# Channel shuffle on one core: eight tiles of 64 KB a partition, permuted inside their slot in pieces of five pixels

## The chip, the core and the metric

The kernel runs on one core of a Trainium2 chip. The metric is device time in microseconds (us), the median of several runs. The profile is one execution of the program, taken by the hardware profiler; its times count from the span's start, at the first instruction. Two engines matter here: VectorE (DVE in the profile), which copies within the on-chip memory (SBUF, 128 partitions), and the 16 DMA engines, which move data between device memory and SBUF. Transfers are issued from two queues: SP issues the loads (q1 in the profile) and ACT issues the stores (q10).

## The reference

The input is a float32 array of 16 x 64 x 64 pixels with 256 channels each, 67.11 MB. The 256 channels of a pixel are 8 groups of 32; the reference transposes the two:

```python
x = x.reshape(batch, h, w, groups, channels_per_group)
x = x.transpose(0, 1, 2, 4, 3)
x = x.reshape(batch, h, w, c)
```

No arithmetic is done. Each pixel's 1 KB stays where it is; inside it, channel g*32 + j goes to place j*8 + g. There are 65,536 pixels, 512 for each partition.

## The kernel before

The pixels are taken in order, in slots. `_SLOTS` (line 12) lists the pixels that each partition gets in a slot: [4, 8], then [28], then twelve times [38], then [16]; 512 in all. The first slot has two parts, each other slot has one. A part of q pixels is a contiguous block of 128 x q pixels of the input, and `rows` cuts it so that each partition's q pixels are one contiguous row of q KB (38 KB in most slots).

For each slot the kernel takes an `in_tile` from a pool of two and an `out_tile` from a pool of three, both sized for 38 pixels (lines 46 and 47). For each part it

- loads the part into `in_tile` by one DMA from the SP queue (line 55),
- copies it into `out_tile` by one VectorE `tensor_copy` (line 57), which reads the source with the order of groups and channels exchanged (a hop of 32 elements between consecutive reads) and writes one contiguous run,
- stores `out_tile` by one DMA from the ACT queue (line 61).

The order on each engine is the order of the program (`manual_schedule`); waits between engines are semaphores that the framework places from the tiles' uses. A load waits until the copy that last read its `in_tile` is done; a copy waits for its load, and for the store that last read its `out_tile`; a store waits for its copy. So loads are released by copies, and the three buffers of `out_tile` keep the stores out of the loads' way.

Of the kernel before, what the change touches and what calls it, by code (L numbers as in the profile page):

```python
# [1 line left out]

# [4 lines left out]


F32 = mybir.dt.float32
P = 128  # L10

_SLOTS = [[4, 8], [28]] + [[38]] * 12 + [[16]]
_IN_BUFS = 2
_OUT_BUFS = 3


@with_exitstack
def kernel(
    ctx: ExitStack,
    tc: tile.TileContext,  # L20
    x: bass.AP,
    groups: bass.AP,
    out: bass.AP,
):
    nc = tc.nc
    b, h, w, c = x.shape
    G = int(groups)
    CPG = c // G
    assert G * CPG == c
    assert sum(map(sum, _SLOTS)) * P == b * h * w  # L30
    biggest = max(map(sum, _SLOTS))

    x_flat = x.rearrange("b h w c -> (b h w c)")
    out_flat = out.rearrange("b h w c -> (b h w c)")

    in_pool = ctx.enter_context(tc.tile_pool(name="in_pool", bufs=_IN_BUFS))
    out_pool = ctx.enter_context(tc.tile_pool(name="out_pool", bufs=_OUT_BUFS))

    def rows(flat, first, q):

        return flat[first * c : (first + P * q) * c].rearrange("(p f) -> p f", p=P)

    ctx.enter_context(tc.manual_schedule(engines=None))
    first = 0
    for parts in _SLOTS:
        in_tile = in_pool.tile([P, biggest * c], F32, name="in_tile")
        out_tile = out_pool.tile([P, biggest * c], F32, name="out_tile")
        at = 0
        pieces = []
        for q in parts:  # L50
            pieces.append((q, first, slice(at * c, (at + q) * c)))
            first += P * q
            at += q
        for q, start, cols in pieces:
            nc.sync.dma_start(out=in_tile[:, cols], in_=rows(x_flat, start, q))  # L55
        for q, start, cols in pieces:
            nc.vector.tensor_copy(  # L57
                out=out_tile[:, cols].rearrange("p (i j g) -> p i j g", j=CPG, g=G),
                in_=in_tile[:, cols].rearrange("p (i g j) -> p i j g", g=G, j=CPG),
            )  # L60
            nc.scalar.dma_start(
                out=rows(out_flat, start, q), in_=out_tile[:, cols]
            )


# [1 line left out]
_INS = ['x', 'groups']  # L67
_OUTS = [((16, 64, 64, 256), 'float32')]

_NUMBERS = {'groups': 8}  # L70


# [26 lines left out]
```

## Time and profile before

| what | value |
|---|---|
| median of 3 runs | 316.17 us (316.07 to 316.84) |
| span of the profiled execution | 314.4 us (its own time is not given beyond the span) |
| VectorE busy | 119.0 us in 16 copies (38% of the span) |
| loads, q1 | 2304 packets, 67.11 MB |
| stores, q10 | 2304 packets, 67.11 MB |
| mean rate over the span | 427 GB/s |
| copy of 38 pixels (128 x 9,728 elements) | 8791 ns |
| copy of 4 pixels (128 x 1,024 elements) | 1092 ns |
| load of 38 pixels, issue to landing | 37.0 us |
| store of 38 pixels, issue to landing | 42.6 us |

The first part of the page gives each engine's busy time. The second cuts the span into 40 equal slices, where a digit is the busy share in tenths. The third gives the DMA queues, with the time of their packets as a share of 16 engines' span. A group of instructions is read as: line, engine, operation, output and input with their shapes, how many; then busy us and mean ns of one; then the idle time of the engine just before them, and what ended it. The chain of waits is read as: start, length, what. A line of the windows gives the stretch, its length, busy time (and instructions) of DVE and POOL, the granted TensorE clock (TensorE is not used), the DMA share and GB/s.

### The profile page before, as it was taken

How to read it: one execution, taken by the hardware profiler on the slowest of the kernel's cores; microseconds unless marked ns; L12 is line 12 of the kernel's file. 1: busy time of each engine (PE TensorE's matmuls, PEld its weight loads, DVE VectorE, ACT ScalarE, POOL GpSimd, SP SyncE). 2: the span in 40 equal slices, each digit the busy share in tenths (PEclk: the TensorE clock that was granted, in tenths of full speed). 3: DMA queues.
4: the chain of work that ended last, by engine and by line, in shares of the span. 5: the costliest groups of instructions: out<-in, count | busy, mean ns of one | idle time of the engine just before them, and what ended most of it. 6: DMA issues, size and time to landing. Idle time of an engine off the chain costs nothing.

```text
span 314.4 us, 132 instructions
## 1 busy us (share of the span) xinstructions
DVE 119.0 (38%) x16; POOL 0.2 (0%) x4
## 2 busy tenths in 40 slices
DVE  2081907309109109019028028037046055065400
POOL 0000000000000000000000000000000000000000
DMA  7999999999999999999999999999999999999997
GB/s 317 405 441 416 435 416 483 401 465 406 450 421 446 426 436 436 401 470 396 475 396 475 396 470 401 470 401 470 401 450 421 446 426 436 436 417 450 429 421 321
DMA packets 4608, 134.22 MB, mean 427 GB/s; under 512 B 512, under 2 KB 512, under 8 KB 768
## 3 DMA queue, kind: packets, MB, share of 16 engines
q1 hardware_dynamic: 2304, 67.11, 49.8%
q10 hardware_dynamic: 2304, 67.11, 49.4%
HBM read 67.11 MB, written 67.11 MB: 427 GB/s over the span
## 4 chain that ended last, share of the span: by engine, by line
DMA 76%; DVE 19%; issue 0%; SPq 0%; DVEq 0%
DMA in_tile<-in_x_dram 76%; DVE out_tile L57 19%; SPq L55 0%; DVEq L57 0%
## 5 line engine op out<-in xcount | busy, mean ns | idle before, releaser
L57 DVE COPY out_tile<-in_tile 128x9728 f32<-128x9728 f32 (+4 forms) x16 | 119.0, 7440 | 179.4 <-DMA in_tile<-in_x_dram 179.4
L80 POOL MEMSET const-uint8-127<- 128x1 uint8 x1 | 0.1, 103 | 0.0
L80 POOL MEMSET const-bfloat16-1.0<- 128x1 bf16 x1 | 0.1, 102 | 0.0
L80 POOL MEMSET const-float32-1.0<- 128x1 f32 x1 | 0.1, 100 | 0.0
L80 POOL MEMSET const-float32-0.0<- 128x1 f32 x1 | 0.1, 99 | 0.2 <-issue 0.2
## 6 DMA issues: line engine op xcount, KB each, us to landing
in_tile<-in_x_dram SPq DMA_DIRECT2D x12, 4864.0 KB, 37.0
out_dram<-out_tile ACTq DMA_DIRECT2D x12, 4864.0 KB, 42.6
in_tile<-in_x_dram SPq DMA_DIRECT2D x1, 3584.0 KB, 14.7
out_dram<-out_tile ACTq DMA_DIRECT2D x1, 3584.0 KB, 30.9
in_tile<-in_x_dram SPq DMA_DIRECT2D x1, 2048.0 KB, 30.4
out_dram<-out_tile ACTq DMA_DIRECT2D x1, 2048.0 KB, 15.2
in_tile<-in_x_dram SPq DMA_DIRECT2D x1, 1024.0 KB, 5.4
out_dram<-out_tile ACTq DMA_DIRECT2D x1, 1024.0 KB, 25.0
```

The lines of the kernel that those rows point to most:

```text
L57: nc.vector.tensor_copy(out=out_tile[:, cols].rearrange("p (i j g) -> p i j g", j=CPG, g=G), in_=in_tile[:, cols].rearrange("p (i g j) -> ...
L80: nc = _bacc.Bacc("TRN2", target_bir_lowering=False, num_devices=1)
```

## The change

The slots become eight tiles of 64 pixels a partition, each loaded by one DMA (64 KB a partition, 8.39 MB) and stored by one. One pool of three slots replaces the two pools. A slot has room for 64 + 5 pixels, 69 KB a partition. The load puts the 64 pixels at pixel 5 and up. VectorE then permutes them inside the slot: each `tensor_copy` takes five pixels and writes them permuted five pixels lower, into room that is free or whose pixels earlier pieces have already read. A tile takes twelve pieces of five pixels (1,280 elements) and one of four (1,024 elements); each piece waits on VectorE's own semaphore for the piece before it. The store takes pixels 0 to 63 of the slot. The next load into a slot waits for the store out of it.

In all there are 8 loads in place of 16, 8 stores in place of 16, and 104 copies in place of 16. The order on SP is the eight loads, on ACT the eight stores, on VectorE the pieces tile by tile. The loads of tiles 0, 1 and 2 wait for nothing; the load of tile k+3 waits for the store of tile k. The source of a piece is 5 x 32 x 8 elements at hops of 256, 1 and 32; its destination is one run of 1,280.

```diff
-_SLOTS = [[4, 8], [28]] + [[38]] * 12 + [[16]]
-_IN_BUFS = 2
-_OUT_BUFS = 3
+_SLOTS = [[64]] * 8
+_BUFS = 3
+
+_SHIFT = 5
...
-    biggest = max(map(sum, _SLOTS))
+    room = max(map(sum, _SLOTS)) + _SHIFT
...
-    in_pool = ctx.enter_context(tc.tile_pool(name="in_pool", bufs=_IN_BUFS))
-    out_pool = ctx.enter_context(tc.tile_pool(name="out_pool", bufs=_OUT_BUFS))
+    pool = ctx.enter_context(tc.tile_pool(name="pool", bufs=_BUFS))
...
-        in_tile = in_pool.tile([P, biggest * c], F32, name="in_tile")
-        out_tile = out_pool.tile([P, biggest * c], F32, name="out_tile")
+        slot = pool.tile([P, room * c], F32, name="slot")
...
-            pieces.append((q, first, slice(at * c, (at + q) * c)))
+            pieces.append((q, first, at))
...
-        for q, start, cols in pieces:
-            nc.sync.dma_start(out=in_tile[:, cols], in_=rows(x_flat, start, q))
-        for q, start, cols in pieces:
-            nc.vector.tensor_copy(
-                out=out_tile[:, cols].rearrange("p (i j g) -> p i j g", j=CPG, g=G),
-                in_=in_tile[:, cols].rearrange("p (i g j) -> p i j g", g=G, j=CPG),
+        for q, start, at in pieces:
+            nc.sync.dma_start(
+                out=slot[:, (at + _SHIFT) * c : (at + _SHIFT + q) * c],
+                in_=rows(x_flat, start, q),
             )
+        for q, start, at in pieces:
+            for lo in range(at, at + q, _SHIFT):
+                n = min(_SHIFT, at + q - lo)
+                src = slot[:, (lo + _SHIFT) * c : (lo + _SHIFT + n) * c]
+                dst = slot[:, lo * c : (lo + n) * c]
+                nc.vector.tensor_copy(
+                    out=dst.rearrange("p (i j g) -> p i j g", j=CPG, g=G),
+                    in_=src.rearrange("p (i g j) -> p i j g", g=G, j=CPG),
+                )
             nc.scalar.dma_start(
-                out=rows(out_flat, start, q), in_=out_tile[:, cols]
+                out=rows(out_flat, start, q), in_=slot[:, at * c : (at + q) * c]
             )
```

## The prediction

> **What bounds the kernel now.** I read the page first: the busy line, the DMA line of the forty slices, the two queues.
>
> ```profile
> DVE 119.0 (38%) x16; POOL 0.2 (0%) x4
> ...
> DMA  7999999999999999999999999999999999999997
> ...
> q1 hardware_dynamic: 2304, 67.11, 49.8%
> q10 hardware_dynamic: 2304, 67.11, 49.4%
> ```
>
> The 16 DMA engines are busy from end to end: loads (q1) and stores (q10) move 67.11 MB each and fill 49.8% + 49.4% of their time. VectorE is busy 38% of the span, and both queues always hold work, so its time is hidden except in the first and last few us. Next, the windows (length, DVE busy, POOL busy, clock, DMA share, GB/s):
>
> ```profile
> 120.00:280.00 160.00, 60.77 (x8) 0.00 (x0) 1.00 1.00 434
> 298.00:306.00 8.00, 0.41 (x1) 0.00 (x0) 1.00 0.99 428
> ```
>
> The first is the middle, where both queues share the engines; the second is the end, where only stores are left. The rate is the same to 1.4%: one queue alone fills the engines. So a byte costs the same whether loads and stores overlap or not, and time is lost only while **both** queues are empty. That is the test for the change. For the fixed cost of a transfer, the list of DMA issues:
>
> ```profile
> in_tile<-in_x_dram SPq DMA_DIRECT2D x1, 512.0 KB, 3.3
> ```
>
> 512 KB at 434 GB/s is 1.2 us, so 2.1 us are fixed; I put 1.05 before the first byte and 1.1 behind the last (an estimate of the split). The copies come from the groups of instructions, shapes kept apart:
>
> ```profile
> L57 DVE COPY out_tile<-in_tile 128x9728 f32<-128x9728 f32 x12 | 105.5, 8791 | 158.5 <-DMA in_tile<-in_x_dram 158.5
> L57 DVE COPY out_tile<-in_tile 128x7168 f32<-128x7168 f32 x1 | 6.6, 6569 | 7.7 <-DMA in_tile<-in_x_dram 7.7
> ...
> L57 DVE COPY out_tile<-in_tile 128x2048 f32<-128x2048 f32 x1 | 2.0, 2019 | 1.5 <-DMA in_tile<-in_x_dram 1.5
> L57 DVE COPY out_tile<-in_tile 128x1024 f32<-128x1024 f32 x1 | 1.1, 1092 | 4.1 <-DMA in_tile<-in_x_dram 4.1
> ```
>
> Between 1,024 and 2,048 elements a copy grows by 0.905 ns an element, between 7,168 and 9,728 by 0.868; what is left at 1,024 is 1092 - 1024 x 0.905 = 165 ns. All idle time in front of copies is a wait for a load. The chain of waits gives the price of one engine step waiting for another:
>
> ```profile
> 30.18 8.83 DVE out_tile L57
> 39.02 0.02 issue
> 39.03 32.20 DMA in_tile<-in_x_dram
> 71.23 0.04 DVEq L57
> 71.27 0.04 issue
> ```
>
> A hand-over around a copy costs 0.02 to 0.08 us. The span is 314.4 us and the median of the runs 316.17; I carry the 1.7 us between them over unchanged.
>
> **The change, part by part.** Bytes: unchanged. A tile is 64 KB x 128 = 8.39 MB; at 434 GB/s 19.3 us, and I take 19.4 alone and 38.8 when the queues share. All 16 transfers are 310.4 us. With 1.75 before the first byte (issue at 0.7, then 1.05) and 1.1 behind the last, the floor of the span is 313.25.
>
> Transfers: 8 + 8 in place of 16 + 16. The 16 fixed costs that go were behind other transfers already (DMA share 1.00), so I cost them at nothing; where a queue runs dry, one costs up to 2.1 us, and it is counted there.
>
> Copies: 16 become 104, 12 pieces of 1,280 elements and one of 1,024 in each tile, each waiting on VectorE's own semaphore for the piece before. I take 0.08 us a hand-over, 1.0 us a tile; no row shows a copy waiting for a copy, so 0 to 0.2 us is the bound. For a piece of 1,280, the low end lies between the rows of 1,024 and 2,048: 1,280 x 0.905 + 165 = 1.32 us, and a tile is V = 12 x 1.32 + 1.09 + 1.0 = **18.0 us**. But every row copies an even number of pixels (4, 8, 28, 38, 16), and the new piece copies five out of a source of 5 x 32 x 8 into one run of 1,280. If the rate of the rows comes from doing two halves side by side, five pixels do not split, and the large rows' rate falls to half: 1,280 x 1.736 + 165 = 2.39 us, V = 12 x 2.39 + 1.09 + 1.0 = **30.8 us**. That is the upper end. The rows are nearer to the low end in size; the odd count is the one thing they do not have, and no row decides. I take the upper end, as my choice, and keep both.
>
> [...]
>
> Order: before, a load waits for the copy of an earlier slot, and stores run beside it from 5 us on. Now a slot is loaded, permuted and stored in place, so load k+3 waits on SP for store k, which waits on ACT for the last piece of tile k. Behind the waiting load SP holds only later loads; behind the waiting store ACT holds only later stores. The schedule with V = 30.8 (us from the span's start):
> - Load 0 lands at 22.2; permute 0 ends at 53.0, permute 1 at 83.8, permute 2 at 114.6, back to back. Load 1 is through at 40.6. Load 2 has the engines alone until store 0 starts at 54.1, has 5.85 us of work left, shares, and ends at 65.8. Store 0 then goes alone and ends at 79.3.
> - Load 3 may start at 79.3 + 1.1 + 1.05 = 81.5, store 1 not before 84.8: both queues are empty for **2.1 us**.
> - Load 3 ends at 116.9, store 1 at 120.3; load 4 runs from 122.5 to 161.2 and store 2 ends at 156.9. From here a store takes 38.8 us shared and ends at 195.8, 234.6, 273.4; each next load is issued while 2 us of work of the one ahead of it remain, so nothing is lost. Load 7 ends at 277.6 and lands at 278.7.
> - Permute 7 runs until 309.6 and store 7 may start at 310.6. Store 6, alone from 277.6, ended at 294.9: **15.7 us** with nothing to move.
> - Store 7 ends at 330.0, the span at 331.1.
>
> Sum: 313.25 + 2.1 + 15.7 = 331.1, and with 1.7 around it **332.8 us**, 5.3% more. The long permute is hidden in the middle, where the other queue covers it, and laid bare behind the last load: before, the last copy (16 pixels) took 3.9 us, beside a store of 38 pixels that was still running; now it is 64 pixels in 13 pieces, and store 6 covers only half of it.
>
> **Rivals.**
> 1. *Pieces at the rate of the rows*, V = 18.0. For it: sizes next to 1,280 are in the trace. Against it: no odd count is. Load 7 ends at 275.5 and permute 7 at 294.6, store 6 ends at 292.8, store 7 starts at 295.6 and ends at 315.0: span 313.25 + 2.8 = 316.1, time 317.8, slower by 0.5%. Up to V = 28 each us of V adds one here.
> 2. *Faster: the permute fits behind store 6.* The place is the drain alone: from the landing of load 7 to the end of store 6 there are 16 us. With V below about 16.1 (a piece below 1.17 us with the same hand-overs) no queue ever runs dry and the span is the floor: 313.25, time 314.95, 0.4% faster, since small transfers at both ends are gone. Against it: 1.17 us is 11% below what the rows give for 1,280 elements; it needs hand-overs near nothing as well.
> 3. *Transfers with rows of 64 KB are slower.* The windows of before differ by 2% (434 to 425 GB/s from 100 to 125 us); with 19.8 us a tile the forecast's schedule ends at 337.1, time 338.8. For it: no row of 64 KB is in the trace. Against it: rows of 38 KB fill the engines to 1.00. [...]
>
> **How the numbers follow.** About 0.3% (1 us, from 315.2 to 317.1) is what can be told from no change. Chances: forecast 0.80, rival 1 0.14, rival 2 0.03, rival 3 0.03. The forecast's own range: hand-overs of 0 to 0.2 us move V from 29.8 to 32.3, 1.9 us in place of 1.1 for landings adds 1.5, and 1% of DMA rate is 3 us: 327 to 340. An odd piece that loses only part of its rate (V = 22) would give 321.9. I take 321 to 340; rivals 1 and 2 and a tail of 0.03 lie outside. Rival 1 reaches from 316.5 (V = 17) to 320, so a third of it counts as no change: same 0.05, faster 0.03, slower 0.92.
>
> **What would show it right or wrong.** Right: 96 pieces near 2.39 us against 8 of four pixels near 1.09; VectorE busy near 238 us; DMA slices full but for a dip near 80 us and an empty stretch of 15 us near 300; one landing of load 7 near 279 and store 7 near 20 us long. Wrong in the piece if the 96 read 1.32 us: VectorE busy near 135 us, and the last gap is 3 us. Wrong in the schedule if slices between 120 and 290 us are not full, or if q1 and q10 alone (before 50 us, after 310 us) fall below 420 GB/s. A piece-to-piece gap over 0.2 us would break the hand-over term.

## The result and the profile after

The changed kernel takes 336.09 us (median of 4 runs, 335.34 to 336.44) against 316.12 us before: a ratio of 1.0625, 95% interval 1.0609 to 1.0642. The profiled execution has a span of 334.7 us and a time of its own of 336.44, so the 1.7 us around the span are as before.

The page after, in its lines on busy time, slices and queues:

```profile
DVE 232.0 (69%) x104; POOL 0.2 (0%) x4
...
DVE  0029999999999208996299925999079971999400
...
DMA  9898989998999999998989999999999998930595
...
q1 hardware_dynamic: 1152, 67.11, 47.3%
q10 hardware_dynamic: 1152, 67.11, 46.5%
```

VectorE is busy 232.0 us in place of 119.0 for the same elements. The DMA line is full until near the end, where slices fall to 3, 0 and 5 while the DVE line reads 9, 9 and 4: the last permute, with nothing to move beside it. The windows (length, DVE busy, POOL busy, clock, DMA share, GB/s) say it in numbers; a packet counts in the window in which it starts:

```profile
2.80:40.00 37.20, 17.08 (x8) 0.00 (x0) 1.00 0.98 425
160.00:280.00 120.00, 87.08 (x39) 0.00 (x0) 1.00 1.00 431
280.00:298.00 18.00, 14.17 (x7) 0.00 (x0) 1.00 0.91 393
298.00:313.00 15.00, 14.79 (x7) 0.00 (x0) 1.00 0.00 0
313.00:334.70 21.70, 0.08 (x1) 0.00 (x0) 1.00 0.90 387
```

In the middle the engines move 431 GB/s, against 434 before. No packet starts from 298 to 313 us, while VectorE works; by the packet records store 6 ends at 300.1 and store 7 starts at 314.0, and nothing moves between the two. In the last window the single store of tile 7 is the only transfer left. The groups of instructions, shapes kept apart, give the piece:

```profile
L64 DVE COPY slot<-slot 128x1280 f32<-128x1280 f32 x96 | 223.5, 2328 | 80.8 <-DMA slot<-in_x_dram 77.7
L64 DVE COPY slot<-slot 128x1024 f32<-128x1024 f32 x8 | 8.8, 1094 | 0.3
```

Five pixels take 2328 ns; four pixels, in the same slots, take 1094. The chain of waits ends with load 7, permute 7 and store 7, one after the other:

```profile
239.15 44.38 DMA slot<-in_x_dram
...
283.62 2.34 DVE slot L64
...
285.98 2.34 DVE slot L64
...
311.97 1.11 DVE slot L64
```

Load 7 is issued at 239.15 and landed for VectorE at 283.6; 13 pieces follow at 2.36 us from start to start.

### The profile page after: what moved, and what is told of

Its sections match the earlier page's. It is cut to its first block, busy times and chain, and to the rows that moved or that the text cites. A ratio compares the mean times of both kernels' runs of the same rounds, so it can differ in the third digit from the quotient of the medians.

```text
span 334.7 us, 183 instructions
## 1 busy us (share of the span) xinstructions
DVE 232.0 (69%) x104; POOL 0.2 (0%) x4
## 4 chain that ended last, share of the span: by engine, by line
DMA 58%; DVE 35%; issue 0%; SPq 0%; DVEq 0%
DVE slot L64 35%; DMA slot<-in_x_dram 33%; DMA out_dram<-slot 25%; SPq L55 0%; DVEq L64 0%
## 5 line engine op out<-in xcount | busy, mean ns | idle before, releaser
L64 DVE COPY slot<-slot 128x1280 f32<-128x1280 f32 (+1 forms) x104 | 232.0, 2233 | 81.0 <-DMA slot<-in_x_dram 77.7
```

Source lines behind the costliest of these rows:

```text
L64: nc.vector.tensor_copy(out=dst.rearrange("p (i j g) -> p i j g", j=CPG, g=G), in_=src.rearrange("p (i g j) -> p i j g", g=G, j=CPG),)
```

## The experiments

Theory A: an odd outermost count of pixels halves the rate of a copy, and the longer permute of the last tile is laid bare behind the last load. Rival B: copying inside one slot is slow in itself. Rival C: the loss lies in the 64 KB transfers. "Excess" below is the time that DMA packets took over their usual length (2.42 us for 64 KB), summed over all packets and divided by 16 engines; it and the moments of first and last packets are read from the trace's packet records.

**Four pixels a piece** (e1_four):

```diff
-_SHIFT = 5
+_SHIFT = 4
```

> Pieces of four pixels, written four pixels lower: 128 copies of 1,024 elements in place of 104, all of an even count. Theory A (an odd count of pixels halves the copy's rate): each piece takes 1.09 us, a tile 16 x 1.09 + 15 x 0.035 = 18.0 us in place of 29.45; the empty stretch behind the last load shrinks by 11.4 us less what was hidden, span 321, time 322.5. Rival B (a copy is slow because it reads and writes one slot, a few pixels apart, each piece behind the last): the pieces stay at 1.82 ns an element, 1.87 us each, a tile stays at 30 us and the time at 336. Rival C (the loss is in the 64 KB transfers, not in the copies): the copies may get faster, the time stays within 2 us of 336.

Measured: 322.58 us, ratio 1.0219 (1.0169 to 1.0269). The group of copies:

```profile
L64 DVE COPY slot<-slot 128x1024 f32<-128x1024 f32 x128 | 140.2, 1095 | 162.0 <-DMA slot<-in_x_dram 157.9
```

The 128 pieces take 1.10 us each inside the slot, so B falls; 13.5 us of the 20 go with the piece alone, so C is not the main cause. The time is as expected. The profiled execution is the slowest of the four (325.51 us), so what is read from its trace is not that of the median.

**Five pixels, walked in another order** (e2_five_j_outer):

```diff
-                    out=dst.rearrange("p (i j g) -> p i j g", j=CPG, g=G),
-                    in_=src.rearrange("p (i g j) -> p i j g", g=G, j=CPG),
+                    out=dst.rearrange("p (i j g) -> p j i g", j=CPG, g=G),
+                    in_=src.rearrange("p (i g j) -> p j i g", g=G, j=CPG),
```

> Same pieces of five pixels, same shift, same bytes; only the order in which a copy walks its elements changes, with the 32 channels of a group outermost (32 x 5 x 8 on both sides) in place of the five pixels. Theory A: the outermost count is even and the same on both sides, so a piece takes 1.28 x 0.905 + 0.165 = 1.32 us, VectorE is busy about 136 us, span 320.4, time 322. Rival B (in place, five pixels apart): 2.33 us a piece and 336 us as before. In between (1.5 to 2.2 us a piece) would say that the writes, now in runs of eight elements, cost something of their own.

Measured: 331.09 us, ratio 1.0476 (1.0456 to 1.0495).

```profile
L64 DVE COPY slot<-slot 128x1280 f32<-128x1280 f32 x96 | 119.9, 1249 | 180.0 <-DMA slot<-in_x_dram 177.0
```

The same five pixels, the same shift, 1249 ns in place of 2328: the order in which the copy walks, not the size, the shift or the slot, sets the rate. This run changes two things at once: the outermost count of the source becomes even (32 in place of 5), and the two sides become equal (32 and 32 in place of 5 and 1,280). That an even count was enough without an equal one is shown by four pixels (4 against 1,024, 1095 ns) above; an odd count equal on both sides was not tried. The time missed its forecast by 9 us. VectorE is nearly idle in the middle of the stretch where this arises; the windows show a slow stretch of DMA (first line this run, second line the changed kernel):

```profile
58.00:80.00 22.00, 0.31 (x1) 0.00 (x0) 1.00 0.95 349
58.00:80.00 22.00, 21.69 (x10) 0.00 (x0) 1.00 0.99 429
```

The engines are busy to 0.95 but move 349 GB/s, in a stretch where VectorE works 0.31 of 22 us. The excess of this run is 8.3 us, against 4.4 in the changed kernel, 2.3 with four pixels and 1.2 before. Three later runs ask why.

**The kernel before with odd counts** (e3_before_odd):

```diff
-_SLOTS = [[4, 8], [28]] + [[38]] * 12 + [[16]]
+_SLOTS = [[4, 8], [28]] + [[37], [39]] * 6 + [[16]]
```

> The kernel before with slots of 37 and 39 pixels in turn in place of twelve of 38: nothing in place, separate tiles, one copy a slot, only the counts odd. Theory A: 1.69 ns an element in place of 0.90, so 16.2 us for 37 pixels and 17.0 for 39, about twice the 8.8 of 38 pixels; VectorE busy near 213 us; since a slot's transfers take 23 us the copies stay hidden and the time stays at 316 within 1 us. Rival B (in place is what is slow): 8.6 and 9.0 us, VectorE busy 119.

Measured: 321.16 us, ratio 1.0157 (1.0116 to 1.0199).

```profile
L57 DVE COPY out_tile<-in_tile 128x9984 f32<-128x9984 f32 x6 | 102.4, 17074 | 42.3 <-DMA in_tile<-in_x_dram 42.3
L57 DVE COPY out_tile<-in_tile 128x9472 f32<-128x9472 f32 x6 | 97.3, 16208 | 35.1 <-DMA in_tile<-in_x_dram 35.1
```

37 pixels take 16.2 us where 38 took 8.8, with separate tiles and one copy a slot. Between the two rows a copy grows by 866 ns for 512 elements, 1.69 ns each. Theory A holds outside the changed kernel too. The forecast of the time failed by 5 us: in the middle the copies are hidden (430 GB/s from 120 to 280 us), but the last copy of 39 pixels, 17 us long, ends at 299.9 us, when both queues have run dry, and its store starts at 300.9, after 1.1 us with nothing to move. The window at the end, in this run and in the kernel before:

```profile
290.00:303.00 13.00, 13.00 (x2) 0.00 (x0) 1.00 0.82 351
290.00:303.00 13.00, 3.87 (x1) 0.00 (x0) 1.00 1.04 451
```

Idle time of the engines grew by 2.7 us against the kernel before and the excess by 1.9; together the 4.6 us between the spans.

**The last tile in three parts** (e4_taper):

```diff
-_SLOTS = [[64]] * 8
+_SLOTS = [[64]] * 7 + [[32, 16, 16]]
```

> The changed kernel with the last tile in three parts of 32, 16 and 16 pixels, each with its own load and store; pieces of five pixels as they are. If the loss is the permute laid bare behind the last load (13 us with both queues empty): the first part is permuted while the others load, the last part's permute takes 7.4 us and ends at about 303, close to the end of the store of tile 6 (300), so the empty stretch goes and the span is 320.5, time 322. Rival C (the 64 KB transfers are slow all along): the time falls by less than 3 us.

Measured: 323.39 us, ratio 1.0236 (1.0219 to 1.0253), with VectorE still busy 232.2 us. The window of the empty stretch:

```profile
298.00:312.00 14.00, 5.60 (x4) 0.00 (x0) 1.00 0.97 418
```

With slow pieces and, for the first seven tiles, 64 KB transfers as they were, 418 GB/s flow where next to nothing did, and 12.7 us are gone. The place of the loss is the end of the last tile. The excess of this run is 6.2 us, more than in the changed kernel.

**All tiles in halves** (e5_halves):

```diff
-_SLOTS = [[64]] * 8
+_SLOTS = [[32, 32]] * 8
```

> The changed kernel with each tile of 64 pixels moved in two halves: two loads and two stores of 32 pixels (32 KB rows), pieces of five pixels as they are (six of five and one of two in each half, so a slot still needs 29.6 us of permute). Theory A with the drain: the last half is permuted in 14.8 us from about 282 to 297 while the store of the half before still runs (to about 303), so both queues never run dry although the pieces stay at 2.33 us; span 315, time 316.7 within 1.5. Second forecast, on the landing: a copy starts behind the last packet of its load by about one packet of the store queue (2.86 us with rows of 64 KB); with 32 KB it starts about 1.6 us behind it. Rival B (slow pieces cost what they cost wherever they stand): over 325.

Measured: 317.31 us, ratio 1.0036 (1.0023 to 1.0048).

```profile
L64 DVE COPY slot<-slot 128x1280 f32<-128x1280 f32 x96 | 223.5, 2328 | 67.9 <-DMA slot<-in_x_dram 65.0
```

The pieces are as slow as ever, to the nanosecond, and 18.8 of the 20 us are gone: the slow piece costs only where no transfer covers it. On the landing: the last load's final packet ends at 285.33 and its copy starts at 287.05, 1.72 us later (1.6 expected).

**Both cuts together** (e6_four_taper): `_SHIFT = 4` and the last tile in 32, 16 and 16.

> Pieces of four pixels (18.0 us of permute a tile) and the last tile in parts of 32, 16 and 16. Both costs taken away together: packets 309.5 us, start and end 3.2, what the packets take over their usual length where the second queue joins 2.3 (the sum seen with four-pixel pieces), span 315.3, time 317.1. If the two cuts were independent and added in full (13.5 and 12.7 us off 336.1), it would be 309.9, which is below the floor of the transfers, so they should not add.

Measured: 324.49 us, ratio 1.0255 (1.0229 to 1.0281). A miss of 7 us; it is even no better than either cut alone. The DMA view of the stretch from 275 to 290 us, where the loads of the last parts run, says why:

```profile
q10 hardware_dynamic: 102, 5.11, 81.8%
q1 hardware_dynamic: 101, 1.46, 22.7%
```

Loads (q1) move 1.46 MB and stores (q10) 5.11 MB, in nearly the same number of packets: the two queues go by turns, one 16 KB row of a load for one row of 64 or 32 KB of a store. The last load of 16 pixels ends at 308.1, where the loads of a whole last tile end at 281.2 with four-pixel pieces. VectorE waits for it, and the last store starts at 315.0; both queues are empty for 0.9 us before it, and from 310 to 320 us the engines idle for 4.4 us in the mean. In e4_taper store 6 was issued 14 us later (274.0 against 260.4), so the loads had the engines to themselves for a while and ended at 292.9, and the slow pieces still had work then: the lag was hidden.

**Four pixels, halves, last tile in 32, 16 and 16** (e7_four_halves_taper):

> Pieces of four pixels, every tile in halves of 32, the last in 32, 16 and 16. No stretch with both queues empty; against the run with whole tiles, shorter rows should halve what packets take over their usual length where the second queue joins: span 314.3, time 316.0, the same as the kernel before within 0.3%. If row length does not matter, 317; if the doubled number of transfers costs, over 318.

Measured: 317.32 us, ratio 1.0035 (1.0021 to 1.0049), 1.3 us above the expectation and nearest to the 317 of "row length does not matter". Yet row length did matter to the excess: no stretch is empty, the excess fell to 1.6 us, from 2.3 with four pixels and whole tiles, and the engines' idle time at start and end is 4.4 us against 3.6 before. VectorE is busy 140.4 us here and 233.4 in e5_halves, and the times are the same.

**The other order, in halves** (e8_j_outer_halves): the edit of e2_five_j_outer and `[[32, 32]] * 8`.

> The copy order with the 32 channels outermost, pieces of five pixels at 1.25 us, every tile in halves. With whole tiles this order gave 331.1 us although VectorE was busy only 128 us: packets took 8 us longer in sum, nearly all between 40 and 100 us, where loads and stores begin to alternate. If that comes from rows of 64 KB in alternation, halves bring it to 4 us or less and the time to 317 to 319. If it comes from this order of copying (its writes go in runs of eight elements), it stays at 8 us with halves and the time at 322 or more.

Measured: 316.98 us, ratio 1.0026 (1.0015 to 1.0038); excess 1.5 us. From 44 to 91 us:

```profile
44.00:91.00 47.00, 21.11 (x19) 0.00 (x0) 1.00 1.01 434
```

With rows of 32 KB the slow stretch is gone (434 GB/s where e2_five_j_outer moved 382 in the same window), with the same order of copying, so that order alone does not cause it. The halves also let the stores join earlier, at 26 us.

**Three pixels in the other order, whole tiles** (e9_three_j_outer): the edit of e2_five_j_outer and `_SHIFT = 3`.

> Whole tiles, the 32 channels outermost, pieces of three pixels (768 elements, 22 a tile): about 0.8 us a piece, 18.3 us a tile, so the first store is issued near 40.9 us, where the four-pixel pieces issued theirs (40.7), and not at 39.0 as with five pixels in this order. It asks what made packets take 8 us longer in that run. If it is the moment in the packets' alternation at which stores join: excess near 2 us as with four-pixel pieces, time 321 to 324. If it is this order of copying: 8 us again and 330 to 332. A count of three is odd too; theory A, that only the outermost count matters, has a piece at 0.8 us, against 1.46 at half rate.

Measured: 322.67 us, ratio 1.0203 (1.0177 to 1.0229); excess 2.1 us.

```profile
L64 DVE COPY slot<-slot 128x768 f32<-128x768 f32 x168 | 136.3, 811 | 160.3 <-DMA slot<-in_x_dram 154.8
```

Three pixels behind an outermost count of 32 take 0.81 us, so the odd number of pixels is harmless where it does not stand outermost. The order of copying is cleared a second time, now with rows of 64 KB.

**Two pixels a piece, whole tiles** (e10_two): `_SHIFT = 2`.

> Whole tiles in the order of the changed kernel, pieces of two pixels (512 elements, 32 a tile): 0.625 us a piece as the trace of the changed kernel's 512-element remainders has it, with 0.035 us between pieces 21.1 us a tile; first store issued near 43.8 us. The empty stretch behind the last load grows by the 3.1 us that a tile takes longer than with four-pixel pieces: 325.5 if packets take 2.3 us over their usual length, up to 331 if they take 8. With the order of copying unlike that of the other run and the moment of joining different from both, an excess over 5 us would speak for the moment.

Measured: 324.35 us, ratio 1.0275 (1.025 to 1.0301); pieces of 0.628 us (those of two pixels in e5_halves took 0.625), excess 2.1 us; the time is 1.2 us under the 325.5 expected, and the empty stretch grew from 4.9 us with four pixels to 6.2, not by 3.1. What singles out e2_five_j_outer with its 8.3 is settled in part: halving the rows took it away (e8_j_outer_halves), the order of copying alone is not it (e9_three_j_outer), and VectorE was mostly idle. Its stores were issued at 39 us, and not at 40.7 or 43.7 as in the runs with about 2 us of excess. But that moment was not varied by itself, and the changed kernel and e4_taper, both from 52 us on, have 4.4 and 6.2. The cause stays open.

No version beats the kernel before; the best in-place one is 0.26% behind it.

## Why the prediction was right, point by point

**The piece.** The upper end, 2.39 us, was taken; 2.328 was measured, since the rate is 1.69 ns an element and not 1.736. Rival 1 (1.32 us) fell in the first group line. The cause behind the choice, the odd outermost count, is shown by three runs: e1_four, e2_five_j_outer, e3_before_odd. The forecast's rate was an estimate, twice the 0.868 ns an element of the even rows; the runs give 1.69 for odd counts (e3_before_odd). That an even count is fast because two halves are done side by side, as the prediction supposes, is shown by no run here; the runs show the counts and the times: 5 against 1,280 outermost took 2328 ns, 32 against 32 took 1249 ns, and 4 against 1,024 took 1095 ns.

**Hand-overs.** 0.08 us was taken, 0.035 measured. A permute is 29.45 us, not 30.8, which gave back 1.35 us behind the last load.

**The schedule.** The order of events held but for one: in the dip store 1 starts first (82.35) and load 3 only at 87.7, not at 81.5. Forecast against measured: permute 1 ends at 83.8 and 81.5, store 0 at 79.3 and 81.5, the dip is 2.1 and 0.9 us, load 7 has landed at 278.7 and 283.6, store 6 ends at 294.9 and 300.1, store 7's first packet is at 310.6 and 314.0, the last at 330.0 and 333.5. The empty stretch was 15.7 us in the forecast and is 13.9. One queue alone stayed above the 420 GB/s that the prediction asked for: 425 from 2.8 to 40 us, and 429 in store 7 (8.39 MB in 19.5 us).

**Where the 3.3 us of the miss went.** Two terms were too small. The transfers: 16 x 19.4 = 310.4 us was the sum, while the packets filled 313.9 us: 309.5 at their usual 2.42 us, and 4.4 of excess, mostly in the first packets after a queue joins the other (near 55 and 85 us). The landing behind the last packet: 1.1 us in the forecast, taken from a load with nothing in the other queue, and 2.86 where the other queue has work (0.37 for load 0, before any store was issued). Along the chain that ends the span, load 7's last packet ends 3.2 us later than forecast (280.8 against 277.6), its landing takes 1.8 us more, and permute 7 takes 1.4 us less; 331.1 became 334.7 in the profiled execution. The range of 321 to 340 had room for both terms. In the total the idle time of the engines came out as forecast, 20.8 us against 20.65, but that is partly luck: the dip and the empty stretch are shorter by 3 us together, and about 3 us of idle time were not in the forecast, because the engines do not end a store together (store 6 ends on them between 296.6 and 300.1 us).

**Rivals 2 and 3.** Rival 2 needed pieces below 1.17 us. Its point of decision (16.1 us a permute) was also set too high: e1_four and e2_five_j_outer had permutes of 18.0 and 16.4 us, 1.9 and 0.3 above it, and left both queues empty for 4.9 and 4.4 us. From the first copy of tile 7 to the end of store 6 there were 14.1 and 12.9 us; the longer landing eats the cover. Rival 3 fell in its own terms: a 64 KB packet takes 2.418 us and a 38 KB packet 1.439, 27.1 and 27.0 GB/s an engine, so the rows themselves are not slower. What the packets took beyond the forecast's sum, 3.5 us, is over half of the 6 us that rival 3 asked for, but it sits where queues join and not in every row.

**What was misjudged outside the forecast.** The forecast's drain has one cure with one price. The runs show about two thirds of the loss gone by either cut (13.5 us by the piece, 12.7 by the taper), nothing more by both, and 18.8 by halves alone.

## What to carry to other kernels

Where transfers fill the whole span, ask which copies no transfer covers. In these runs a copy's speed counted there alone, mostly behind the last load: with VectorE busy 233.4 us (e5_halves) and 140.4 us (e7_four_halves_taper) the time was 317.3 both times. A smaller transfer in both queues was worth more than a faster copy: halves with slow pieces took off 18.8 us of the 20, whole tiles with fast pieces 13.5. Cut both queues to the same row size: in e6_four_taper they went by turns packet for packet (101 packets with 1.46 MB and 102 with 5.11 MB from 275 to 290 us), and small last loads beside large stores gained nothing over the fast piece alone (324.49 us against 322.58). Where a copy has an odd count outermost, try another order of its dimensions: the five pixels that took 2328 ns took 1249 with the 32 channels outermost on both sides. Before a tile is made larger, ask what is then left behind the last landing and what still covers it.

## What the runs showed of the hardware that was not expected

- A load's copy started later where stores ran beside the load: from its last row to its copy 2.86 us with 64 KB rows (the changed kernel; 2.42 us a packet), 1.93 with 38 KB (the kernel before; 1.44), 1.72 with 32 KB (e5_halves; 1.21), and 0.37 for the first load of the changed kernel, with no store issued yet. The 4-byte packet that ends a load lies behind its last row by 2.42, 1.44 and 1.21 us, as long as one packet of the other queue each time.
- In e6_four_taper, from 275 to 290 us, the two queues shared the engines packet for packet, not byte for byte: rows of 16 KB beside rows of 64 and 32 KB got 1.46 MB against 5.11 MB, in about 90 rows each.
- Packets took longer than usual by 2.1 to 8.3 us in sum with 64 KB rows, 1.5 to 1.7 with 32 KB, 1.2 in the kernel before and 3.1 in it with odd counts. Of each, 0.5 to 0.7 us falls in the first 10 us. In the changed kernel 3.3 of its 4.4 us follow within some 10 us of a queue joining the other; in e2_five_j_outer 7.1 of its 8.3 us lie between 40 and 100 us. The cause is open.
- A five-pixel copy with the 32 channels outermost takes 1249 ns, less than the 1.32 us interpolated from the even copies of the old order, although its writes go in runs of eight elements.
